# Value and output projections of two mixers as 2x2 block products with seven partial products, full-height diff scores, and a causal mask on GpSimd

## The chip, the cores and the metric

The kernel runs on one core of a Trainium2 chip. A core has a matrix engine (TensorE, in the profile PE, its weight loads PEld), a vector engine (VectorE, DVE), an engine for activation functions (ScalarE, ACT), a general one (GpSimd, POOL), and SyncE (SP), which here issues every transfer between DRAM and the on-chip memory SBUF. TensorE writes into PSUM, eight banks of 128 x 512 float32. The metric is the device time of one execution in microseconds (us).

## The reference

The reference is a two-layer decoder trunk on one sequence of 1024 tokens with 1024 features, in float32. Each layer is feed-forward, mixer, feed-forward, each between two RMS norms and added to the residual. Cut to what matters here:

```python
def hybrid_mixer(h, w_in, w_out, ...):          # layer 0
    proj = h @ w_in                              # 1024 x 3088
    dq, dk, dv, gq, gk, gv, gg, ga = split(proj) # 512 512 512 256 256 512 512 16
    a_out = diff_attention(dq, dk, dv, ...)      # 4 heads, two scores each (64 deep), values 128 wide
    o_b = gla_chunked(gq, gk, gv, log_a)         # 4 heads of linear attention, values 128 wide
    return concatenate([a_out, norm(o_b) * silu(gg)]) @ w_out

def stick_breaking(h, w_qkv, w_out):             # layer 1, 8 heads of 128
    q, k, v = split(h @ w_qkv, 3)
    ...
    mask = key < query                           # strict
    log_keep = where(mask, -softplus(z), 0)
    att = where(mask, exp(z + log_keep + suffix_sums(log_keep)), 0)
    return (att @ v) @ w_out
```

Diff attention takes softmax(score 0) - lambda * softmax(score 1) for each head, with a mask that lets a token see itself, then an RMS norm of each head's output.

## The kernel before

Every large matmul works on float32 split in two parts, `hi` and `lo` (ACT writes `hi`, VectorE `lo`, in `split`, `split_w` and `split_tile`), and takes three passes, hi·hi, hi·lo and lo·hi (`mm3`, lines 228 to 230). Tokens are worked in two halves of 512 (`TB`), features in tiles of 128 (`P`). X, the normalized input of a stage, lies transposed: eight tiles of 128 features by 512 tokens for each half.

The feed-forward stages (`gu`, `down_strassen`) already treat their products as 2x2 blocks with seven partial products (Strassen's scheme in Winograd's form): sums of X blocks on VectorE, sums of weight blocks on GpSimd, 12 quarter-size matmuls for each contraction tile. The mixers don't.

A mixer begins with `first_proj`: the first head's q and k for the first token half, then `make_x` transposes the second half's X, then the same for it. The rest of the projections are closures that the attention loops call as filler: `proj_steps` gives two steps for a 128-column tile (one for each token half, 24 matmuls 512 wide), `proj_v_steps` four for 256 value columns (48 matmuls 256 wide, with tokens as the output rows; line 771 evicts two row tiles at a time into `v`). `filled(fill, i)` spreads what is left of a head's fillers evenly over its eight blocks of 128 queries. The order of instructions on each engine is set by the framework at build time: by program order, with instructions that it expects to be ready moved ahead of those that would wait.

Layer 0 runs linear attention in two pairs of heads (`gla_pair`: a decay by gate, then seven levels in which VectorE, GpSimd and ACT make factors, TensorE multiplies and VectorE copies under a mask, then the state chain and the output), then diff attention in four heads. `diff_attn` makes for each query block and each of the two components the scores (`scores`, line 788), with two passes: one 128 rows deep that holds hi parts of q and k and lo parts of q, and one 64 rows deep for the lo part of k (`k[2]`, one tile for both components). Then come maxima (VectorE), exponentials (ACT), their combination (VectorE), transposes (line 803), the product with `v` (line 924) and the norm. Layer 1 runs eight heads of `sb_attn`: scores with three passes, two sigmoids on ACT (lines 820 and 821), a reversed running product (line 823, `TENSOR_TENSOR_SCAN`) and a product (826) on VectorE, transposes, and the product with `v` (831). In both, the causal mask is a fourth matmul on the block of the diagonal (line 791), which adds -1e30 from a bfloat16 tile.

Each head's output, transposed (`ot`, 128 x 1024), goes to DRAM (`put_o`), the last one stays. The output projection (`out_steps`, `mix_out`) runs in four parts of eight contraction tiles, 96 matmuls each: first token half by first column half in seven fillers of the last head, the rest after it. The first half's norm, residual and next X (`epilogue`, `make_x`) lie under the second half's matmuls. Weights pass through four raw buffers (`rp`, 4 KB a partition) into six split ones (`wp`).

## Time and profile before

| | us |
|---|---|
| median of 3 runs | 2507.36 (2505.67 to 2509.91) |
| the profiled execution | 2509.04 |
| its span in the profile | 2507.3 |
| granted TensorE clock in it | 0.994 of full speed |
| ACT busy | 1069.0 (43%) |
| first feed-forward | to about 361 |
| layer 0: first projections, linear, diff attention | 361 to 875 |
| layer 0: rest of the output projection | 875 to 965 |
| two feed-forwards | 965 to 1625 |
| layer 1: stick-breaking attention | 1625 to 2095 |
| layer 1: rest of the output projection | 2095 to 2182 |
| last feed-forward | 2182 to 2507 |

The stages overlap by some microseconds. In the rows below, a group of instructions is written as line, engine, operation, what is written `<-` what is read, shape and count, then `busy us, mean ns of one | idle time of the engine just before them, and what ended it`. A timeline row has the start, the duration, and the same names; a duration is that of one record (of all, where a row stands for several), and records of one engine may overlap, since the engines are pipelined. A row of the table of windows has the stretch, its length, the busy time and count of each engine, the granted clock, the share of the transfer engines and what they moved in GB/s.

### The profile page before, as it was taken

The page shows a single profiled execution, that of the slowest core. Times are in us where ns is not written, and L with a number is a line of the kernel's source. Part 1 is how long each engine was busy: PE and PEld are TensorE (multiplying, and loading weights), DVE is VectorE, ACT ScalarE, POOL GpSimd, SP SyncE. Part 2 cuts the span into 40 slices and gives each one's busy share as a digit, 9 for nine tenths or more (in the row PEclk, how much of TensorE's full clock was granted, in tenths as well). Part 3 has the DMA queues.
Part 4 walks back from the last instruction along what each step waited for, and adds up shares of the span by engine and source line. Part 5 has one row for each costly group of instructions (what it writes and reads, how often), then busy time and mean ns, then how long its engine had stood idle before and what let it go on. Part 6 is the DMA issues. An engine that isn't in the chain of part 4 may idle for free.

```text
span 2507.3 us, 32918 instructions
## 1 busy us (share of the span) xinstructions
PE 2430.2 (97%) x12253; PEld 1995.7 (80%) x12253; DVE 1733.3 (69%) x2635; ACT 1069.0 (43%) x2143; POOL 671.2 (27%) x542
## 2 busy tenths in 40 slices
PE   7999999999999999999989999999999999999998
PEld 6887878788777678887868887788888988888776
DVE  6768786653656758777888678855546476686778
ACT  6423454322545646323455234543323254552343
POOL 2545431110000012545423455310000000043553
PEclk9999999999999999999999999999999999999999
DMA  5321651211100354233463225531111024422245
GB/s 171 84 81 61 213 185 47 68 46 65 34 30 35 105 184 128 76 85 108 161 197 84 78 65 187 170 101 34 41 36 35 30 100 160 151 83 84 63 158 196
DMA packets 238842, 251.97 MB, mean 100 GB/s; under 512 B 9861, under 2 KB 186201, under 8 KB 238681
## 3 DMA queue, kind: packets, MB, share of 16 engines
q1 hardware_dynamic: 238680, 249.85, 31.3%
q8 instruction: 97, 1.59, 0.3%
q14 instruction: 65, 0.52, 0.1%
HBM read 215.21 MB, written 34.60 MB: 100 GB/s over the span
## 4 chain that ended last, share of the span: by engine, by line
PE 82%; DVE 10%; issue 3%; POOL 2%; ACT 2%; DMA 2%; DVEq 0%; SPq 0%; POOLq 0%; ACTq 0%
PE z L788 4%; PE pps L228 4%; PE pps L230 4%; PE pps L229 4%; PE pd L228 3%; PE pd L230 3%; PE pd L229 3%; PE pa L230 3%; PE pa L228 3%; PE pa L229 3%; PE pc L229 3%; PE pc L230 3%; PE pc L228 3%; PE vps L228 3%; PE po L831 2%
## 5 line engine op out<-in xcount | busy, mean ns | idle before, releaser
L182 POOL TENSOR_TENSOR rs<-ms,nhalf 128x1 f32<-128x1 f32 (+1 forms) x136 | 100.2, 743 | 1046.1 <-DVE ms L180 950.4
L277 ACT CAST wq<-rawt 128x512 fp32r<-128x512 f32 x264 | 163.3, 621 | 351.4 <-PE pc L230 164.3
L278 DVE TENSOR_TENSOR wq<-rawt,wq 128x512 fp32r<-128x512 f32 x264 | 242.8, 924 | 22.6 <-ACT wq L277 16.7
L219 DVE TENSOR_TENSOR hl<-rawd,hl 128x512 fp32r<-128x512 f32 x200 | 166.2, 834 | 86.6 <-ACT hl L218 86.3
L218 ACT CAST hl<-rawd 128x512 fp32r<-128x512 f32 x200 | 123.7, 621 | 208.5 <-issue 46.7
L228 PE MATMUL pps<-hl,wh 128*128 128x512 f32 x512 | 206.6, 404 | 0.3 <-DVE hl L222 0.3
L230 PE MATMUL pps<-hl,wl 128*128 128x512 f32 x512 | 203.1, 397 | 0.0
L229 PE MATMUL pps<-hl,wh 128*128 128x512 f32 x512 | 202.7, 396 | 0.0
L371 POOL TENSOR_TENSOR rawt<-rawt 128x512 f32<-128x512 f32 x44 | 72.0, 1636 | 395.9 <-DMA rawt<-in_ffn_w_up_dram 184.9
L228 PE MATMUL pd<-hl,wq 128*128 128x512 f32 x352 | 139.9, 397 | 10.7 <-DVE c L385 10.7
L228 PE MATMUL vps<-vh,hl 128*128 128x256 f32 x512 | 146.9, 287 | 0.0
L805 DVE COPY att<-tps 128x512 f32<-128x512 f32 (+2 forms) x96 | 56.4, 587 | 129.6 <-PE tps L803 129.0
L230 PE MATMUL vps<-vh,hl 128*128 128x256 f32 x512 | 145.1, 283 | 0.0
L229 PE MATMUL vps<-vl,hl 128*128 128x256 f32 x512 | 144.8, 283 | 0.0
L228 PE MATMUL pa<-hl,wq 128*128 128x512 f32 x352 | 138.7, 394 | 4.1 <-DVE hl L222 3.4
L230 PE MATMUL pa<-hl,wq 128*128 128x512 f32 x352 | 138.1, 393 | 4.1 <-DVE wq L278 4.1
L788 PE MATMUL z<-k,q 128*128 128x512 f32 (+5 forms) x444 | 140.0, 396 | 1.8 <-ACT b L821 1.0
L228 PE MATMUL pc<-hl,wq 128*128 128x512 f32 x352 | 137.6, 391 | 3.1 <-ACT hl L218 3.1
L230 PE MATMUL pd<-hl,wq 128*128 128x512 f32 x352 | 139.6, 396 | 0.0
L229 PE MATMUL pd<-hl,wq 128*128 128x512 f32 x352 | 139.4, 396 | 0.0
L230 PE MATMUL pc<-hl,wq 128*128 128x512 f32 x352 | 138.3, 393 | 0.0
L229 PE MATMUL pc<-hl,wq 128*128 128x512 f32 x352 | 138.3, 393 | 0.0
(281 smaller groups left out, 6684.4 us busy)
## 6 DMA issues: line engine op xcount, KB each, us to landing
rawt<-in_ffn_w_gate_dram SPq DMA_DIRECT2D x88, 512.0 KB, 4.0
rawd<-in_ffn_w_down_dram SPq DMA_DIRECT2D x60, 512.0 KB, 3.7
rawd<-in_ffn_w_down_dram SPq DMA_DIRECT2D x116, 256.0 KB, 2.7
rawt<-in_ffn_w_up_dram SPq DMA_DIRECT2D x44, 512.0 KB, 4.0
hres<-h SPq DMA_DIRECT2D x40, 512.0 KB, 2.9
h<-hres SPq DMA_DIRECT2D x40, 512.0 KB, 5.1
rawt<-in_hyb_w_in_dram SPq DMA_DIRECT2D x16, 512.0 KB, 3.9
rawt<-in_sb_w_qkv_dram SPq DMA_DIRECT2D x16, 512.0 KB, 3.8
```

What stands on the lines that cost most here:

```text
L182: nc.gpsimd.tensor_tensor(out=rs, in0=ms, in1=self.nhalf.to_broadcast([P, n]) if n > 1 else self.nhalf, op=ALU.pow)
L218: nc.scalar.copy(out=t[:, 0], in_=src)
L219: nc.vector.tensor_tensor(out=t[:, 1], in0=src, in1=t[:, 0].bitcast(F32), op=ALU.subtract)
L228: nc.tensor.matmul(ps, lhsT=ah, rhs=bh, start=first, stop=False, skip_group_check=more)
L229: nc.tensor.matmul(ps, lhsT=ah, rhs=bl, start=False, stop=False, skip_group_check=more)
L230: nc.tensor.matmul(ps, lhsT=al, rhs=bh, start=False, stop=last, skip_group_check=more)
L277: nc.scalar.copy(out=w[:, 0], in_=src)
L278: nc.vector.tensor_tensor(out=w[:, 1], in0=src, in1=w[:, 0].bitcast(F32), op=ALU.subtract)
L371: gt(out=b11, in0=b12, in1=b11, op=ALU.subtract)
L788: nc.tensor.matmul(z[:, :wide], lhsT=lhs[:, i * P:(i + 1) * P], rhs=rhs[:, c0:c0 + wide], start=j == 0, stop=j == len(passes) - 1 and not ...
L805: (nc.scalar.copy if j0 else nc.vector.tensor_copy)(out=t[:, :n], in_=ps[:, :n])
L831: nc.tensor.matmul(po, lhsT=v[:, j, hv:hv + P], rhs=at, start=j == 0, stop=j == i)
```

## The change

*Value rows.* A new stage `values` runs at the start of each mixer, in place of `first_proj`. It computes the 1024 value columns (layer 0: 512 of diff attention and 512 of linear attention) for all tokens as a 2x2 block product, and stores the rows in a DRAM tile `vd`. `load_v` fetches 256 columns (1 MB) as they are needed. `proj_v_steps` is gone from all fillers, and `proj_steps` gives four half steps of 12 matmuls instead of two of 24. `Blocks` loads weight blocks and forms the sums t1 to t4 on GpSimd (1, 2, 1 and 3 operations).

```diff
+class Blocks:
+    def load(self, *places):
+        r = self.t.rp.tile([P, 2, TB], F32, name="rawd", tag="raw")
+        for i, (k, c) in enumerate(places):
+            self.t.nc.sync.dma_start(out=r[:, i], in_=self.w[self.rows(k), self.cols[c]])
+        return r
...
+    def t1(self, j):
+        r = self.load((j, 0), (j, 1))
+        self.sub(r[:, 0], r[:, 1], r[:, 0])
+        return r[:, 0]
+    def t2(self, j):
+        r = self.t1(j)
+        b = self.b22(j)
+        self.sub(b, b, r)
+        return b
...
+    def t4(self, j):
+        r = self.t1(j)
+        b = self.load((j + self.KH, 0), (j + self.KH, 1))
+        self.sub(b[:, 0], b[:, 0], b[:, 1])
+        self.sub(r, b[:, 0], r, ALU.add)
+        return r
...
+    def values(self, l, w, cols, X, xn1, vd):
...
+        pa = self.new_accs("va")
+        self.rows_product(pa, A[0:4], weights(B.b11), True)
+        for t in range(NTT):
+            nc.scalar.copy(out=u2[t], in_=pa[t])
+        self.rows_product(pa, A[4:8], weights(B.b21), False)
+        for t in range(NTT):
+            out(0, 0, t, lambda o: nc.scalar.copy(out=o, in_=pa[t]))
...
+        R = self.make_raw(xn1, "mix_pre_g", l, xr)
+        X.append([self.split(r, self.hp) for r in R])
...
+        for j in range(4):
+            tt(out=s12[j], in0=R[j], in1=R[j + 4], op=ALU.add)
+            S1.append(self.split(s12[j], sp))
+            tt(out=s12[j], in0=s12[j], in1=hi(j), op=ALU.subtract)
+            tt(out=s12[j], in0=s12[j], in1=lo(j), op=ALU.subtract)
+            S2.append(self.split(s12[j], sp))
+        pb = self.new_accs("vb")
+        self.rows_product(pb, S2, weights(B.t2), True)
+        for t in range(NTT):
+            tt(out=u2[t], in0=pb[t], in1=u2[t], op=ALU.add)
+        pc = self.new_accs("vc")
+        self.rows_product(pc, S1, weights(B.t1), True)
...
+        self.rows_product(pc, S4, weights(B.b22), False)
...
+        pd = self.new_accs("vd")
+        self.rows_product(pd, S3, weights(B.t3), True)
...
+        self.rows_product(pd, X[1][4:8], weights(B.t4), False)
```

*Output projection.* `out_steps` now gives eight fillers of 12 matmuls: the products A11·b11 and S3·t3 (S3 = first minus second token half). `mix_out` loads the seven stored heads again (`orw`), forms S1, S2 and S4 on GpSimd and runs the other five products, b21, t2, t1, b22 and t4, with the first half's norm and next X between the last two.

```diff
+        for j in range(4):
+            gt(out=o[j][1], in0=o[j][1], in1=o[j + 4][1], op=ALU.add)
+            gt(out=o[j][0], in0=o[j][1], in1=o[j][0], op=ALU.subtract)
+        pa = self.new_accs("oa")
+        product(pa, lambda j: o[j + 4][0], B.b21, True)
...
+        product(pb, lambda j: o[j][0], B.t2, True)
...
+        product(pc, lambda j: o[j][1], B.t1, True)
...
+        product(pc, lambda j: o[j + 4][0], B.b22, False)
...
+        for t in range(NTT):
+            gt(out=c22[t], in0=c22[t], in1=p7[t], op=ALU.add)
+            gt(out=u2[t], in0=u2[t], in1=p7[t], op=ALU.add)
+        xn0 = self.epilogue(0, fo[0], ss[0], False, hsrc, hdst, False)
+        nxt0 = self.make_x(xn0, gname, gi, self.xp)
+        pd = self.new_accs("od")
+        product(pd, lambda j: o[j + 4][1], B.t4, True, tail=4)
```

*Scores.* In diff attention the lo part of k gets a tile of its own for each component, filled in both row halves (one more ACT copy for each, 16 in all), and the second pass is 128 rows deep. In stick-breaking attention the mask matmul goes; GpSimd writes the diagonal block of both sigmoids instead.

```diff
-                zs = self.scores([(q[c], k[c]), (q[c][r], k[2][r])], i, "incl")
+                zs = self.scores([(q[c], k[c]), (q[c], k[2 + c])], i, "incl")
...
-            zs = self.scores([(q[:, 0], k[:, 0]), (q[:, 0], k[:, 1]), (q[:, 1], k[:, 0])], i, "strict")
+            zs = self.scores([(q[:, 0], k[:, 0]), (q[:, 0], k[:, 1]), (q[:, 1], k[:, 0])], i, None)
...
+            for t, fill_with in ((a, 1.0), (b, 0.0)):
+                nc.gpsimd.affine_select(out=t[:, n - P:n], in_=t[:, n - P:n], pattern=[[-1, P]],
+                                        compare_op=ALU.is_ge, fill=fill_with, base=-1, channel_multiplier=1)
```

Besides, the tile of post-norm gains moves to a pool of its own and some constants share a buffer; in `gla_pair` the fillers are spread evenly over its four output pieces.

More of the change, by code (lines that the diff above doesn't have):

```diff
@@ L671, in down_strassen, with rows_product @@
         return nxt0, self.epilogue(1, fo1, ss[1], True, hsrc, hdst, nxt is None)
+    def rows_product(self, accs, As, Bs, start, tail=1):
+        n = len(As)
+        m = max(0, n - tail)
+        seq = [(j, t) for j in range(m) for t in range(NTT)] + [(j, t) for t in range(NTT) for j in range(m, n)]
+        for j, t in seq:
+            ts = slice(t * P, (t + 1) * P)
+            self.mm3(accs[t], As[j][:, 0, ts], As[j][:, 1, ts], Bs[j][:, 0], Bs[j][:, 1],
+                     start and j == 0, j == n - 1, more=not start)
@@ L1045, in gla_pair @@
                                         .to_broadcast([P, 4, P]), op=ALU.mult)
-                fill[2 * h + c4]()
+                for _ in range(len(fill) // (4 - 2 * h - c4)):
+                    fill.pop(0)()
                 pt = self.zp.tile([P, 4, P], F32, name="got", tag="z")
@@ new lines, in out_steps, with mix_out @@
+        self.begun = B, order, st
+        return [lambda n=n: step(n) for n in range(8)]
+    def mix_out(self, l, hsrc, hdst, gname, gi):
+        nc = self.nc
+        tt, gt = nc.vector.tensor_tensor, nc.gpsimd.tensor_tensor
+        B, order, st = self.begun
+        C = B.cols
+        wp = self.wp_tag()
+        pg = self.load_pg(self.a["mix_post_g"][l])
+        cx = ExitStack()
+        orw = self.dyn(cx, "orw", KD - 1)
+        o = []
+        for j in range(KD):
+            if j == KD - 1:
@@ L1198, in prep @@
                 r = self.olast
             else:
-                r = self.rp.tile([P, S], F32, name="rawo", tag="raw")
-                self.nc.sync.dma_start(out=r, in_=self.ot[l][order[f]])
-            for tb in range(2):
-                O[tb].append(self.split(r[:, tb * TB:(tb + 1) * TB], self.hp if tb else self.xp))
-        accs = []
-        def step(f):
-            if not accs:
-                accs.extend(self.acc.tile([P, TB], F32, name="dps%d" % t, tag="acc") for t in range(NTT))
-            prep(f)
-            self.down_step(w, order[f], O[0], f, KD, accs)
@@ new lines, in product @@
+        def product(accs, a, b, start, tail=1):
+            As, Bs = [], []
+            for j in range(4):
+                As.append(self.split(a(j), self.hp))
+                Bs.append(self.split(b(j), wp))
+            self.rows_product(accs, As, Bs, start, tail)
+        for j in range(4):
+            gt(out=o[j][1], in0=o[j][1], in1=o[j + 4][1], op=ALU.add)
+            gt(out=o[j][0], in0=o[j][1], in1=o[j][0], op=ALU.subtract)
+        pa = self.new_accs("oa")
+        product(pa, lambda j: o[j + 4][0], B.b21, True)
@@ L1227, in mix_out @@
+        for t in range(NTT):
+            c = fo[1][t][:, C[0]]
+            tt(out=c, in0=pd[t], in1=u2[t], op=ALU.add)
+            gained(c, 1, t, 0)
+        xn1 = self.epilogue(1, fo[1], ss[1], False, hsrc, hdst, False)
+        cx.close()
+        self.octx.close()
         self.hctx.close()
```

284 lines of the change are left out of this document (181 added, 103 removed).

## The prediction

> **What bounds the kernel now.** I read the first part of the page, then the groups by line, then TensorE's timeline for the real pace of its matmuls, then VectorE's timeline beside GpSimd's, and last the table of windows for the stages that change.
>
> ```profile
> span 2507.3 us, 32918 instructions
> PE 2430.2 (97%) x12253; PEld 1995.7 (80%) x12253; DVE 1733.3 (69%) x2635; ACT 1069.0 (43%) x2143; POOL 671.2 (27%) x542
> ```
>
> TensorE is busy for 97% of the span, so the first question is what the change does to its queue. The durations of the groups mislead here, because a matmul's record runs past the start of the next one. The pace is the distance between starts:
>
> ```profile
> L228 PE MATMUL vps<-vh,hl 128*128 128x256 f32 x512 | 146.9, 287 | 0.0
> L228 PE MATMUL dps<-hl 128*128 128x512 f32 x256 | 101.9, 399 | 0.0
> 361.41 0.39 PE L228 MATMUL pps<-hl,wh 128*128 128x512 f32 x1
> ...
> 372.10 0.39 PE L230 MATMUL pps<-hl,wl 128*128 128x512 f32 x1
> ...
> 597.60 0.28 PE L229 MATMUL vps<-vl,hl 128*128 128x256 f32 x1
> ...
> 603.12 0.28 PE L230 MATMUL vps<-vh,hl 128*128 128x256 f32 x1
> ```
>
> The first pair is the first and last of 48 matmuls 512 wide: 10.69 us over 47 steps, 0.2274 us each. The second is the first and last of 47 that are 256 wide: 5.52 us over 46 steps, 0.120 us. So the 256-wide value projection, whose duration of 287 ns looks dear beside 399 ns, is only 5% dearer per column.
>
> **TensorE's part of the sum.** Value projection: three groups (L228 to L230) of 512, 1536 matmuls at 0.120 us, 184.3 us. After: seven products of 4 row tiles by 4 contraction tiles by 3 passes, 336 matmuls a layer, 672 at 0.2274 us, 152.8 us. Saved: **31.5 us**, not the 170 us that durations would suggest. Output projection: 768 matmuls (three groups of 256) become 672, 96 x 0.2274 = **21.8 us** saved.
>
> ```profile
> L788 PE MATMUL z<-k,q x192: 274/436/505, 635.6 to 874.9; 128*128 128x512 f32 x40, 64*128 64x512 f32 x40, 128*128 128x256 f32 x32, 64*128 64x256 f32 x32
> 722.34 1.42 PE L788 MATMUL z<-k,q 128*128 128x384 f32 x4
> 723.69 0.23 PE L791 MATMUL z<-mkb_incl,identb 128*128 128x128 bf16 x1
> ...
> 2066.61 1.14 PE L788 MATMUL z<-k,q 128*128 128x384 f32 x6
> 2067.59 0.23 PE L791 MATMUL z<-mkb_strict,identb 128*128 128x128 bf16 x1
> 2067.63 0.48 PE L228 MATMUL dps<-hl 128*128 128x512 f32 x1
> ```
>
> Diff scores: of 192 matmuls half contract 64 rows only. At 722.34 a block of 640 keys takes two full and two 64-row passes (384 and 256 wide) and 1.35 us; at 2066.61 stick-breaking attention takes the same widths in six full passes and 0.98 us, 0.163 us a pass. So each 64-row pass costs (1.35 - 4 x 0.163) / 2 = 0.35 us more than a full one. With K=128 everywhere, 96 x 0.35 = **33.5 us** go. The Trainium skill ("TensorE: Matmul & The Clock Gate", section "Why this matters for your kernels") says that a single K=32 matmul takes as long as a K=128 one; by that nothing would go. The rows above disagree.
>
> Mask: 64 matmuls leave stick-breaking attention, 0.04 us each (2067.59 to 2067.63): **2.6 us**.
>
> ```profile
> PE xps L210 <- DVE xn L193: 4.3, 5, 1.7
> 40.41 3.49 PE xps L268 x32
> ```
>
> The mixers' second half of X is transposed 32 times before and after (3.5 us), but now the first product needs the first half alone and stands ahead of it for 96 x 0.2274 = 21.8 us, so that wait goes: **4 us**. TensorE's queue together: 31.5 + 21.8 + 33.5 + 2.6 + 4 = **93 us** less.
>
> **What the seven products ask of VectorE and GpSimd.** This is where I expect much of it to be given back.
>
> ```profile
> 319.19 1.88 DVE L648 TENSOR_TENSOR fo<-dc,u 128x512 f32<-128x512 f32 x3
> ...
> 263.54 0.68 DVE L219 TENSOR_TENSOR hl<-ph,hl 128x512 fp32r<-128x512 f32 x1
> 263.86 1.51 POOL L566 TENSOR_TENSOR rawd<-rawd 128x512 f32<-128x512 f32 x1 [0.79 <-DVE hl L219]
> ...
> 264.21 1.71 DVE L219 TENSOR_TENSOR hl<-t,hl 128x512 fp32r<-128x512 f32 x1
> ```
>
> Three 512-wide VectorE operations in a row take 1.88 us: a pace of (1.88 - 0.68) / 2 = 0.60 us. One that reads two SBUF operands while GpSimd works takes 1.71 us instead of 0.68, 1.03 us more, and ends about when GpSimd's ends. What that costs on average is seen in the feed-forward down products, which already have this form:
>
> ```profile
> L219 DVE TENSOR_TENSOR hl<-rawo,hl 128x512 fp32r<-128x512 f32 x28 | 18.4, 684 | 0.0
> L219 DVE TENSOR_TENSOR hl<-rawd,hl 128x512 fp32r<-128x512 f32 x200 | 166.2, 834 | 86.6 <-ACT hl L218 86.3
> L219 DVE TENSOR_TENSOR hl<-ph,hl 128x512 fp32r<-128x512 f32 x136 | 125.4, 934 | 0.0
> L566 POOL TENSOR_TENSOR rawd<-rawd 128x512 f32<-128x512 f32 x40 | 57.7, 1451 | 36.9 <-DMA rawd<-in_ffn_w_down_dram 34.3 <-DVE hl L219 2.4
> ```
>
> Against 684 ns without GpSimd (rawo), 200 x 0.150 + 136 x 0.250 = 64 us were added; the code has 35 GpSimd operations in each down stage (10 of L566), 140 in all. That is 0.46 us per GpSimd operation, my value, since that stage is the nearest; the ends are 0.2 and 1.03.
>
> *Values stage, each layer.* VectorE has 52 splits, 28 combinations and 20 PSUM evictions, 100 operations; 92 of them come after the second half of X is there: 55.2 us, and 28 GpSimd operations add 12.9, so 68 us. TensorE then has some 5 us of the first product left, the transposes, and five products of 48 matmuls (10.9 us each): 63 us. Stall 5 us, two layers **10 us** (ends 0 and 42). What is late there is S2 for the third product: it waits behind eight splits of X and the S1 tiles.
>
> *Output stage, each layer.*
>
> ```profile
> L475 DVE SCALAR_TENSOR_TENSOR h<-fo,rs,h 128x1024 f32<-128x1024 f32 x32 | 42.9, 1359 | 10.7 <-POOL rs L182 10.7
> L193 DVE TENSOR_SCALAR fo<-h,rs 128x1024 f32<-128x1024 f32 x28 | 21.1, 753 | 10.0 <-POOL rs L182 9.7
> L222 DVE SCALAR_TENSOR_TENSOR hl<-xps,gcol,hl 128x512 fp32r<-128x512 f32 x64 | 43.3, 743 | 2.5 <-ACT hl L221 2.5
> 905.00:965.00 60.00, 59.53 (x276) 48.80 (x275) 38.60 (x71) 33.45 (x65) 9.31 (x13) 1.00 0.58 186
> ```
>
> The window shows the stage now: TensorE never waits, VectorE is at 64%, and the 192 matmuls of the second row half, 43.7 us, hide the first half's normalization. After: 40 splits, 20 evictions, 16 gains at 0.60 us (45.6), eight rows of 1.36 + 0.75 (16.9), eight splits of the next X (5.9), 68.4 us, and 44 GpSimd operations add 20.2: 88.6 us. Seven splits and ten GpSimd operations (8.8 us) can go ahead of the last head's end, and twelve operations and four rows of the second half (15.6 us) can lie under the feed-forward's first columns. Left: 64.2 us, against 5 x 10.9 + 3.5 - 8.2 (three quarters of the first product done as filler) = 49.9 us. Stall 14 us, two layers **29 us** (ends 7 and 67). It falls between the last two products: only t4's 10.9 us cover the first half's normalization. The seven loads of the stored heads go to SP ahead of the weights; what is left of their landing I count in the upper end.
>
> *Transfers.* A values stage loads 56 x 256 KB and stores 16 x 256 KB, 18.9 MB in some 85 us, 222 GB/s.
>
> ```profile
> 250.00:260.00 10.00, 10.00 (x46) 8.29 (x45) 5.48 (x9) 5.27 (x10) 2.57 (x2) 1.00 0.81 290
> ```
>
> 290 GB/s is seen without a wait of TensorE, so I cost it at nothing; four raw buffers, two to a t4, are the cover, and if they don't do, each t4 costs its load and three GpSimd operations instead of 2.7 us. The value rows go through DRAM: each 1 MB comes back one head pair early, or under the eight half steps of the first projections (21.8 us), so that costs nothing too; bare, it would be 3.6 us at that rate, eight times.
>
> **The attention stages lose filler.**
>
> ```profile
> 400.00:425.00 25.00, 25.00 (x199) 23.91 (x199) 16.40 (x33) 11.75 (x18) 2.10 (x2) 1.00 0.07 22
> 440.00:465.00 25.00, 23.61 (x133) 19.92 (x134) 21.35 (x27) 6.96 (x8) 2.24 (x2) 1.00 0.13 43
> 650.00:905.00 255.00, 250.77 (x1338) 189.00 (x1338) 167.13 (x394) 137.44 (x383) 19.58 (x33) 1.00 0.18 63
> L730 ACT CAST k<-pps 64x512 fp32r<-64x512 f32 x16 | 9.3, 581 | 7.1 <-DVE k L713 6.9
> L127 POOL TENSOR_SCALAR_AFFINE_SELECT mk_strict<-mk_strict 128x128 f32<-128x128 f32 x1 | 0.3, 319 | 0.0
> 2078.17 0.63 PE L803 MATMUL tps<-ident,b 128*128 128x128 f32 x4 [0.63 <-DVE b L826]
> ...
> 2085.88 0.30 PE L803 MATMUL tps<-ident,b 128*128 128x128 f32 x1 [0.90 <-DVE b L826]
> ```
>
> Linear attention: the 25 us at 400 are covered by value matmuls that leave. The gate projections, now in the next stretch, can come forward, and that stretch is VectorE's anyway (21.35 of 25). I take **6 us** (ends 0, and 16 if the 16.4 us of VectorE's chain lie bare). Diff attention: TensorE falls from 255 us to about 200 (33.5 us of short passes and 23 us of values go), VectorE stays near 165 and ACT gets 16 more casts of 0.581 us; half of those (5 us) and two waits a head as in the last two rows, 6 us, make **11 us** (ends 0 and 28). Stick-breaking attention: the last head, which is filled with 12 matmuls a block as all heads will be, waits 0.63 + 0.90 us; seven heads 10.7 us. Its queue is fuller than the others' will be, but the two selects (0.32 us) now stand in the chain before the scan, and the scans and transposes queue behind them. **8 us** (ends 0 and 20).
>
> **The sum.** The profiled execution took 2509.0 us, 1.7 above its span; the median shown is 2507.4. Saved 93, given back 10 + 29 + 6 + 11 + 8 = 64: 29 less, 2480 in that execution's terms and **2478** against the median.
>
> **The rivals.** *A, all is covered.* VectorE's backlog sinks under the projections behind the values stage and under the feed-forward; the attention costs (25 us) stay: 2507.4 - 93 + 25 = 2439. For it: the down products run with hardly a wait. Against: they have five or six contraction tiles per eviction, these have four. *B, slower: the port.* If VectorE stands for the whole of nearly every GpSimd operation, 1.03 us, the values stage is 84 us against 63 and the output stage 83.6 against 49.9: stalls 42 and 67, and with 25 that is 134 against 93, 2548. The sign turns at 0.70 us per GpSimd operation, since each 0.1 costs 12 us. For it: 264.21. Against: the mean of 0.46. The Trainium skill ("SBUF — State Buffer", section "Who interferes with whom") states B's rule, an exclusive pair that an operation holds to its end; the single rows agree, the mean shows how seldom they meet. *C, K=128 saves nothing* (the change doesn't do what it says there, because the dear part is changing operands, not the 64 rows): 2478 + 33.5 = 2511. *D, the attention stages starve:* their upper ends, 64 instead of 25, 2517.
>
> **How the numbers follow.** The forecast has 0.48, with a range of its own of 2445 to 2510; A 0.14, B 0.16, C 0.06, D 0.11, and 0.05 is something else. A measurement of this kernel tells about 0.2%, 5 us. Faster: 0.43 + 0.14 + 0.03 + 0.03 = 0.63; same 0.09; slower 0.28. The range goes from A (2438) to just below B (2535).
>
> **What would show it.** Right: the 64-row passes gone from the scores, and blocks of diff attention 0.7 us (up to 512 keys) or 1.4 us shorter; TensorE idle before S2's product on `hl` from VectorE, and before the last product or its transposes; VectorE near 90% in both stages, its two-operand splits well over 0.684 us. Wrong: TensorE waiting on DMA in the output stage, VectorE under 80% there, or idle time in most heads of stick-breaking attention.

## The result, and the profile after

The forecast was wrong in sign. The changed kernel takes **2645.0 us** (median, 2639.9 to 2645.8) against 2508.6 beside it: a ratio of 1.054, 95% interval 1.052 to 1.056. That is 136 us slower, and outside the range of 2438 to 2535.

The first part of the page of the changed kernel, each engine's busy time, share of the span and instructions:

```profile
span 2644.1 us, 32215 instructions
PE 2386.2 (90%) x11229; PEld 1930.7 (73%) x11229; DVE 1933.5 (73%) x2866; ACT 1130.2 (43%) x2263; POOL 996.6 (38%) x820
```

TensorE has 1024 matmuls fewer and is busy 44 us less, while the span grew by 137: it now waits. VectorE's share rises only from 69% to 73%. Nothing on this page looks like a bound; the stages do.

In this table a stage begins with its first matmul in the trace. "Beyond the pace" is its length less its matmuls at the paces of the prediction (0.227 us at 512 columns, 0.120 at 256, and likewise 0.172 at 384, 0.11 at 128 and 0.04 for the bfloat16 matmuls of the mask); it is what TensorE waits or loses.

| stage | before, us | beyond the pace | after, us | beyond the pace |
|---|---|---|---|---|
| layer 0: first projections; after, with values | 28.4 | 3.0 | 137.8 | 36.1 |
| linear attention | 245.8 | 26.8 | 180.7 | 30.8 |
| diff attention | 252.5 | 47.5 | 219.0 | 44.0 |
| output projection behind the last head | 63.6 | 1.6 | 104.0 | 45.8 |
| layer 1: first projections; after, with values | 51.7 | 3.3 | 138.2 | 36.4 |
| stick-breaking attention | 414.6 | 24.0 | 382.6 | 61.8 |
| output projection behind the last head | 72.6 | 1.6 | 103.2 | 45.0 |

The four feed-forwards keep their length within 3 us. In the mixers the matmul time falls by 26.6 + 29.2 = 55.8 us; what lies beyond it grows by 192.1.

The waits view of the changed kernel, for TensorE: what it waited for, us in total, times, the longest:

```profile
PE xps L262 <- DVE fo L245: 47.5, 7, 23.4
PE vb L280 <- ACT hl L270: 34.3, 3, 16.6
PE tps L919 <- DVE b L946: 30.2, 32, 4.9
PE oc L280 <- DVE c L1400: 17.7, 2, 9.3
...
PE vd L280 <- DVE vo L811: 9.4, 2, 4.7
PE oa L280 <- ACT hl L270: 6.9, 2, 6.3
```

Six rows hold 146 us. In the profile before, the waits of the first and third for the same VectorE operations come to 3.2 us, and the others aren't there. `vb` is the second product of the values, `oc` the third product of the output, `xps` the transposes for the next X behind the output's first half, `tps` the transposes of the weights in stick-breaking attention.

The timeline of the changed kernel around these waits, first in the values stage, then in the output stage (start, duration, engine, line, what is written; idle before it in brackets):

```profile
394.37 2.50 DVE L781 TENSOR_TENSOR s<-xr 128x512 f32<-128x512 f32 x4 [2.83 <-ACT xr L322]
396.79 8.12 DVE L271 TENSOR_TENSOR hl<-xr,hl 128x512 fp32r<-128x512 f32 x8
404.83 0.68 DVE L271 TENSOR_TENSOR hl<-s,hl 128x512 fp32r<-128x512 f32 x1
...
408.63 0.79 PE L280 MATMUL vb<-hl 128*128 128x512 f32 x1 [16.48 <-ACT hl L270]
...
938.65 7.48 POOL L61 TENSOR_TENSOR rawd<-rawd 128x512 f32<-128x512 f32 x4 [10.00 <-DMA rawd<-in_hyb_w_out_dram]
945.59 1.09 DVE L271 TENSOR_TENSOR hl<-rawd,hl 128x512 fp32r<-128x512 f32 x1 [4.36 <-ACT hl L270]
946.60 2.47 DVE L1400 TENSOR_TENSOR c<-oc,u 128x512 f32<-128x512 f32 x4
947.42 0.76 PE L280 MATMUL oc<-hl 128*128 128x512 f32 x1 [8.33 <-DVE c L1400]
958.70 6.87 POOL L61 TENSOR_TENSOR rawd<-rawd 128x512 f32<-128x512 f32 x5
966.25 0.69 DVE L271 TENSOR_TENSOR hl<-rawd,hl 128x512 fp32r<-128x512 f32 x1 [3.14 <-ACT hl L270]
967.47 1.88 DVE L1404 TENSOR_TENSOR fo<-oc,u 128x512 f32<-128x512 f32 x3
...
983.50 0.90 PE L262 MATMUL xps<-ident,fo 128*128 128x128 f32 x3 [22.68 <-DVE fo L245]
```

Two things are to be seen. At 394, eight splits of X (8.12 us where they would take 4.9 at 0.60 each) and the sums stand between the second half's X and the product that needs only S2. At 945 and 966, VectorE's queue is in order: the eviction at 946.60 belongs to matmuls of which the last began at 938.7, but a weight split is ahead of it that waits, through ScalarE, for GpSimd's sums. The evictions at 967.47, of matmuls of which the last began at 960.4, are late for the same reason, and only then does the residual and norm chain start, 16 us long, to the transposes at 983.50.

The same stretches in the table of windows (busy us of each engine, granted clock, DMA share, GB/s), of the changed kernel:

```profile
360.00:490.00 130.00, 101.36 (x431) 80.19 (x431) 86.23 (x129) 47.21 (x84) 55.66 (x38) 0.91 0.61 191
392.00:445.00 53.00, 34.25 (x140) 26.71 (x139) 48.79 (x69) 24.74 (x45) 21.00 (x9) 0.84 0.35 112
445.00:498.00 53.00, 48.24 (x201) 38.94 (x200) 17.29 (x26) 8.46 (x12) 18.25 (x14) 0.94 0.82 249
392.00:408.60 16.60, 0.15 (x2) 0.00 (x0) 14.23 (x19) 10.92 (x22) 5.57 (x4) 0.62 0.48 161
408.60:413.00 4.40, 4.37 (x10) 3.06 (x11) 4.40 (x8) 0.72 (x2) 3.35 (x1) 0.51 0.44 142
890.00:1002.00 112.00, 71.12 (x301) 57.54 (x302) 74.08 (x106) 42.97 (x90) 59.68 (x45) 0.80 0.48 166
897.00:904.00 7.00, 0.33 (x1) 0.14 (x1) 0.41 (x1) 0.86 (x2) 1.59 (x2) 0.79 1.00 382
```

VectorE is at 66% in both stages (86 of 130, 74 of 112) and TensorE at 78% and 64%: neither fills the stage. But VectorE's work lies unevenly: 48.8 of the 53 us behind the second half's X, 17.3 of the next 53. The last row is the start of the output stage: all engines nearly idle, TensorE for 6.3 us, and the transfers full at 382 GB/s, while the stored heads and the first weights come in together.

### The profile page after: what moved, and what is told of

The parts are those of the page before. It is cut to its first block, busy times and chain, and to the rows that moved or that the text cites. A ratio compares the mean times of both kernels' runs of the same rounds, so it can differ in the third digit from the quotient of the medians.

```text
span 2644.1 us, 32215 instructions
## 1 busy us (share of the span) xinstructions
PE 2386.2 (90%) x11229; PEld 1930.7 (73%) x11229; DVE 1933.5 (73%) x2866; ACT 1130.2 (43%) x2263; POOL 996.6 (38%) x820
## 4 chain that ended last, share of the span: by engine, by line
PE 55%; DVE 15%; issue 12%; POOL 8%; DMA 6%; ACT 3%; SPq 1%; POOLq 0%; DVEq 0%; ACTq 0%
DVE hl L271 4%; PE pd L280 3%; PE pd L281 3%; PE pd L282 3%; PE pc L281 3%; PE pc L282 3%; PE pc L280 3%; POOL rawd L61 3%; PE pa L282 3%; PE pa L280 3%; PE pa L281 3%; POOL rs L234 2%; PE pps L280 2%; PE pps L282 2%; PE pps L281 2%
## 5 line engine op out<-in xcount | busy, mean ns | idle before, releaser
L271 DVE TENSOR_TENSOR hl<-rawd,hl 128x512 fp32r<-128x512 f32 x248 | 218.9, 886 | 139.2 <-ACT hl L270 138.8
L270 ACT CAST hl<-rawd 128x512 fp32r<-128x512 f32 x248 | 153.3, 622 | 345.6 <-POOL rawd L61 144.9
L234 POOL TENSOR_TENSOR rs<-ms,nhalf 128x1 f32<-128x1 f32 (+1 forms) x136 | 105.8, 785 | 410.6 <-DVE ms L232 340.2
L330 DVE TENSOR_TENSOR wq<-rawt,wq 128x512 fp32r<-128x512 f32 x264 | 240.5, 916 | 12.2 <-ACT wq L329 6.3
L61 POOL TENSOR_TENSOR rawd<-rawd 128x512 f32<-128x512 f32 x112 | 177.4, 1591 | 177.9 <-DMA rawd<-in_sb_w_qkv_dram 47.2
L280 PE MATMUL pd<-hl,wq 128*128 128x512 f32 x352 | 139.8, 397 | 10.7 <-DVE c L437 10.7
L280 PE MATMUL pa<-hl,wq 128*128 128x512 f32 x352 | 139.4, 396 | 3.2 <-DVE hl L274 3.2
L282 PE MATMUL pa<-hl,wq 128*128 128x512 f32 x352 | 138.6, 395 | 3.5 <-DVE wq L330 3.2
L281 PE MATMUL pa<-hl,wq 128*128 128x512 f32 x352 | 138.5, 394 | 0.0
L940 POOL TENSOR_SCALAR_AFFINE_SELECT a<-a 128x128 f32<-128x128 f32 x64 | 24.5, 384 | 285.0 <-ACT a L936 263.2
L904 PE MATMUL z<-k,q 128*128 128x512 f32 (+2 forms) x480 | 125.8, 374 | 4.4 <-ACT e L1019 3.7
L271 DVE TENSOR_TENSOR hl<-ph,hl 128x512 fp32r<-128x512 f32 x136 | 126.5, 941 | 0.0
```

What stands on the lines that cost most here:

```text
L61: self.t.nc.gpsimd.tensor_tensor(out=out, in0=a, in1=b, op=op)
L234: nc.gpsimd.tensor_tensor(out=rs, in0=ms, in1=self.nhalf.to_broadcast([P, n]) if n > 1 else self.nhalf, op=ALU.pow)
L270: nc.scalar.copy(out=t[:, 0], in_=src)
L271: nc.vector.tensor_tensor(out=t[:, 1], in0=src, in1=t[:, 0].bitcast(F32), op=ALU.subtract)
L280: nc.tensor.matmul(ps, lhsT=ah, rhs=bh, start=first, stop=False, skip_group_check=more)
L281: nc.tensor.matmul(ps, lhsT=ah, rhs=bl, start=False, stop=False, skip_group_check=more)
```

## The experiments

Four kernels first split the change into its parts.

**k128**: before, with only the diff scores' second pass 128 rows deep (and what makes room for the tiles: the gains tile and some constants move, and one pool of the attention goes from four buffers to three).

```diff
-            zs = self.scores([(q[c], k[c]), (q[c][r], k[2][r])], i, "incl")
+            zs = self.scores([(q[c], k[c]), (q[c], k[2 + c])], i, "incl")
...
+                self.nc.scalar.copy(out=L[c][o, cs], in_=L[c][r, cs].bitcast(F32))
```

> The kernel before with only the second pass of the diff scores made 128 rows deep (a lo tile of k for each component, eight k buffers, and the moves of the gains tile and constants that make room). If a 64-row pass costs 0.35 us more than a full one and TensorE bounds diff attention: about 2476 us (-33). If what was dear was the change of operands and not the 64 rows: 2508. If the casts on ACT and the shorter cover take half of it back: 2490.

Measured: 2488.2 us, ratio 0.992 (0.991 to 0.994): 19 us faster. Diff attention falls from 252.5 to 231.6. The block of 640 keys that the prediction priced, in the timeline of this kernel:

```profile
712.62 0.83 PE L790 MATMUL z<-k,q 128*128 128x384 f32 x4
713.29 0.23 PE L793 MATMUL z<-mkb_incl,identb 128*128 128x128 bf16 x1
```

Four passes in 0.67 us, where they took 1.35: 0.34 us for each short pass, the unit price of the prediction. But all recorded score passes of the stage together, from one start to the next, fall from 68.0 to 43.2 us, 24.8, not 33.5. A pair of passes gains 0.28 us on average at 256 and 384 columns and only 0.22 at 512, and 40 of the 96 pairs are 512 wide. At 256 columns the medians before were 0.294 us for the full pass of a pair and 0.313 for the short one; here they are 0.200 and 0.122. And the stage gains less than its passes: 2.5 of its 20.9 us are matmuls of the output projection that now run behind the last head. Beyond the pace, the first three heads fall by 19.1 us, the last, whose fillers are those output steps, not at all (13.1 before, 13.7 here).

**mask**: before, with only the causal mask of stick-breaking attention on GpSimd.

```diff
-            zs = self.scores([...], i, "strict")
+            zs = self.scores([...], i, None)
...
+            for t, fill_with in ((a, 1.0), (b, 0.0)):
+                nc.gpsimd.affine_select(out=t[:, n - P:n], in_=t[:, n - P:n], ...)
```

> The kernel before with only the mask of stick-breaking attention on GpSimd (two selects for each block, no mask matmul). Serial-chain theory: the selects lie ahead of the scan, but the 24-matmul fillers of the kernel before cover them, so 2506 to 2511. Small-step theory, with the mask as its main part: the stage goes from 415 us towards the 383 + 92 of the changed kernel's, so 2520 to 2535.

Measured: 2506.6 us, ratio 0.9996 (0.9986 to 1.0006), no difference. The stage goes from 414.6 to 411.7 us, about the 2.6 us of its mask matmuls; the selects in the chain cost nothing that shows.

**outonly**: before, with only the new output projection (`out_steps`, `mix_out`, `Blocks`). **oldout**: the changed kernel with the old output projection.

> The kernel before with only the output projection as seven products. Serial-chain theory: the stretch from the last head to the next feed-forward grows by 40 us in layer 0 and 31 us in layer 1 as in the changed kernel, so 2580 us. Rival (the output stage only suffers from what the other parts left behind): under 2530.

> The changed kernel with the old output projection. If the loss of that part is its own, 2645 - 75 = 2570 us; if the parts share one bound (VectorE with GpSimd on its port), less comes back: over 2600.

Measured: outonly 2603.3 us, ratio 1.038 (1.037 to 1.040), 96 us slower, 23 more than its first expectation; oldout 2545.1, ratio 1.015 (1.013 to 1.016), 37 us slower and below both of its expectations. With 19 for k128 that makes the values stage and what goes with it 57 us slower. The parts add up: 96 + 57 - 19 = 134, of 136. Both block products lose; the output loses more.

The next four ask why.

**nosum**: the changed kernel without the sums of weight blocks.

```diff
     def sub(self, out, a, b, op=ALU.subtract):
-        self.t.nc.gpsimd.tensor_tensor(out=out, in0=a, in1=b, op=op)
+        pass
```

> The changed kernel with the sums of weight blocks on GpSimd left out: each product reads the first raw block in place of the sum (the values are then not the reference's). All loads, splits, matmuls and evictions stay. Chain theory (TensorE idles because the work between two products is a serial chain on VectorE and ScalarE with no matmuls beside it): the 16.6 us gap before the second product of the values and most of the 22.8 us gap before the transposes in the output stage stay, because their chains hold few GpSimd sums; the 8.5 us gap inside the third output product goes, since that chain ran through a late sum; 2600 to 2625 us. Port theory (112 GpSimd sums of 1.59 us take VectorE's time one for one, and VectorE is the bound of both stages): nearly all of the extra idle time of these stages goes, some 2 x 33 + 2 x 44 us, less what the matmuls need: 2500 to 2530 us.

Measured: 2572.0 us, ratio 1.026 (1.025 to 1.028). The 112 sums cost 73 us, 0.65 each. Between the two theories: the values stages fall by 16.6 and 15.9 us, the output stages by 8.2 and 14.2, stick-breaking attention by 10.8; in layer 0 the wait before `vb` falls only from 16.5 to 12.2 us, the one before the transposes from 22.7 to 21.9, and the one inside the third output product from 8.3 to 2.2. So the sums are half of the loss, and the two long waits are mostly something else.

**vlate**: the changed kernel with the splits of the second half's X behind the third product's eviction.

```diff
-        X.append([self.split(r, self.hp) for r in R])
...
         for t in range(NTT):
             tt(out=c22[t], in0=pc[t], in1=u2[t], op=ALU.add)
+        X.append([self.split(r, self.hp) for r in R])
```

> The changed kernel with one thing in the values stage later: the eight splits of the second token half's X are written behind the third product's eviction, instead of ahead of the sums that the second product needs. Same work. Chain theory: the gap before the second product falls from 16.6 us to some 9 us in each mixer, as these splits took 8.1 us in front of it; 2 x 7 us less, 2628 to 2636 us. Port theory: VectorE and GpSimd have the same work in the stage, and the stage keeps its length within 3 us: 2640 to 2648 us.

Measured: 2648.7 us, ratio 1.056 (1.054 to 1.058): no gain. The wait before `vb` falls from 16.5 to 11.7 us, somewhat less than the chain theory has it, and the stage stays at 138.6 us in layer 0: six waits of 1.0 to 2.6 us stand in the later products, 10.2 in all, where the changed kernel has three of 6.9 together, and the rest comes back as slower matmuls. The chain theory fails here. Its timeline shows what VectorE meets while GpSimd sums:

```profile
393.98 1.75 DVE L271 TENSOR_TENSOR hl<-rawd,hl 128x512 fp32r<-128x512 f32 x1
395.65 1.75 DVE L782 TENSOR_TENSOR s<-s,hl 128x512 f32<-128x512 f32 x1
397.32 1.75 DVE L271 TENSOR_TENSOR hl<-rawd,hl 128x512 fp32r<-128x512 f32 x1
399.00 0.68 DVE L783 TENSOR_TENSOR s<-s,hl 128x512 f32<-128x512 f32 x1
```

Three GpSimd sums run from 393.62 to 398.53. Each VectorE operation that starts beside them takes 1.75 us, the next one 0.68.

**oswap**: the changed kernel with the last output product ahead of the first half's residual and norm.

```diff
+        pd = self.new_accs("od")
+        product(pd, lambda j: o[j + 4][1], B.t4, True, tail=4)
+        xn0 = self.epilogue(0, fo[0], ss[0], False, hsrc, hdst, False)
         for t in range(NTT):
             gt(out=c22[t], in0=c22[t], in1=p7[t], op=ALU.add)
             gt(out=u2[t], in0=u2[t], in1=p7[t], op=ALU.add)
-        xn0 = self.epilogue(0, fo[0], ss[0], False, hsrc, hdst, False)
         nxt0 = self.make_x(xn0, gname, gi, self.xp)
-        pd = self.new_accs("od")
-        product(pd, lambda j: o[j + 4][1], B.t4, True, tail=4)
```

> The changed kernel with the last output product (48 matmuls, 10.9 us) placed ahead of the first token half's residual and norm chain, and the eight GpSimd additions of the seventh product behind that chain's start. Same work. Chain theory: these 10.9 us of matmuls now run beside the chain, and the 22.8 us gap before the transposes falls by 8 to 14 us, shared with a new wait for the last product's operands; 2 x 8 to 2 x 14 us less, 2615 to 2630 us. Port theory: VectorE and GpSimd have the same work, the stage keeps its length within 3 us: 2639 to 2648 us.

Measured: 2644.0 us, ratio 1.055 (1.053 to 1.057): nothing. The waits view for TensorE in this stage of oswap:

```profile
PE xps L262 <- DVE fo L245: 7.1, 2, 6.5
...
PE pa L280 <- DVE hl L274: 2.7, 1, 2.7
PE od L280 <- ACT hl L270: 2.4, 1, 2.4
```

The wait before the transposes falls from 22.7 to 6.5 us, most of it by the product's own 10.9, which now lies there; the stage gains 5 us (104.0 to 98.7, 103.2 to 98.4), and the feed-forwards behind it lose 3.9 and 2.4. Behind layer 0 most of it is lost in the first 40 us: after a wait of 2.7 us before `pa` (in the rows above) eight of the next matmuls come some 0.43 us apart instead of 0.227. That the second half's chain has lost its cover doesn't show: its transposes wait 1.2 us here and 0.9 in the changed kernel.

**late**: oldout with q and k in whole steps of 24 matmuls.

```diff
-        return [lambda tb=tb, kh=kh: step(tb, kh) for tb in range(2) for kh in range(2)]
+        return [lambda tb=tb: (step(tb, 0), step(tb, 1)) for tb in range(2)]
```

> The changed kernel with the old output projection (2545.1 us before this edit), and the projections of q and k given to the attention loops in whole steps of 24 matmuls again, so that the spreading rule places four of them at the last four query blocks of a head instead of a half step at each of the eight. Same matmuls. Placement theory (the stick-breaking attention lost its time because the last blocks, whose chains are longest, now have 12 matmuls to cover them instead of 24): the two waits of 1.3 us per head at the last blocks shrink, stick-breaking attention falls from 365 us by 10 to 18 us, diff attention by 0 to 4; 2525 to 2535 us. Cover theory (the value projections that left the loops are missed as cover wherever the rest is placed): waits move to the early blocks, and the time stays within 4 us of 2545. GpSimd theory (the mask on GpSimd and the extra copies are what holds it): no change either.

Measured: 2533.7 us, 11.4 less than oldout; stick-breaking attention 365.3 to 351.6. The placement theory holds. TensorE's wait in the same stretch of the stage, first oldout, then late:

```profile
PE tps L919 <- DVE b L946: 21.0, 28, 1.1
```

```profile
PE tps L919 <- DVE b L946: 3.4, 8, 1.1
```

Four steps over eight query blocks fall on the last four, whose chains are long; eight half steps fall one on each block, and the last blocks have 2.7 us of cover for a chain that needs more.

Three more weigh the price of the sums.

**t2keep**: the changed kernel with the second product's sums kept for the fourth operand.

```diff
     def t4(self, j):
-        r = self.t1(j)
-        b = self.load((j + self.KH, 0), (j + self.KH, 1))
-        self.sub(b[:, 0], b[:, 0], b[:, 1])
-        self.sub(r, b[:, 0], r, ALU.add)
+        r = self.load((j + self.KH, 0))[:, 0]
+        self.sub(r, r, self.kept[j])
         return r
```

> The changed kernel with the second product's weight sums kept, so that the last product's operand is one load and one GpSimd sum instead of two loads and three sums: per product of seven, 8 of 28 sums and 4 x 3 of the loads of 256 KB in the last product go (to pay for the room, the values stage has 3 row buffers on their way to DRAM instead of 4). With all sums left out the changed kernel took 2572.0 us, 73 less; 8 of 28 of that is 21 us. GpSimd theory (each sum costs about its share, through the port and through late operands): 2615 to 2630 us, and VectorE's wait ahead of the last product's splits in the values stage, 4.8 us of TensorE in each mixer, goes. Chain theory (the two long gaps of 16.6 and 22.8 us are other chains, and the sums of the last product lie beside them): 2635 to 2645 us.

Measured: 2607.7 us, ratio 1.040 (1.039 to 1.042): 37 us less, more than the 21 of its share and below both expected ranges. The output stages fall by 12.0 and 7.3 us, stick-breaking attention by 9.4. The wait in the values' last product, which was to go, falls from 4.7 to 2.7 us in layer 0 and stays at 4.6 in layer 1. The wait before the transposes falls from 22.7 to 14.6 us, because the evictions ahead of the norm no longer come late. That need not be the work of the sums, since this edit takes away loads too. In nosum, with no sums at all, the same evictions came 6 us after their last matmul began (930.06), behind a weight split of the next feed-forward that waited for its load:

```profile
935.07 0.62 ACT L329 CAST wq<-rawt 128x512 fp32r<-128x512 f32 x1 [5.42 <-DMA rawt<-in_ffn_w_gate_dram]
935.72 0.69 DVE L330 TENSOR_TENSOR wq<-rawt,wq 128x512 fp32r<-128x512 f32 x1 [5.35 <-ACT wq L329]
936.32 1.88 DVE L1404 TENSOR_TENSOR fo<-oc,u 128x512 f32<-128x512 f32 x3
```

So VectorE's queue makes the evictions late in both kernels, once behind t4's sums (958.70), once behind a load. With the sums on VectorE and all loads in place (vsum, below) the wait is 16.3 us. What stands ahead of the evictions changes from build to build, and no run divides t2keep's gain between fewer sums and fewer loads.

**vsum**: the changed kernel with the sums on VectorE.

```diff
-        self.t.nc.gpsimd.tensor_tensor(out=out, in0=a, in1=b, op=op)
+        self.t.nc.vector.tensor_tensor(out=out, in0=a, in1=b, op=op)
```

> The changed kernel with the 112 weight sums on VectorE instead of GpSimd, one word of the code. On GpSimd a sum takes 1.59 us and stretches a VectorE operation beside it from 0.68 to 1.75 us; on VectorE it takes about 0.6 us. Port theory (the sums cost VectorE more from the neighbour than they would on itself): VectorE's time in the two stages falls by 112 x 0.4 = 45 us, and the time by 20 to 40 us: 2605 to 2625. Load theory (VectorE is the bound, and any work added to its queue lengthens the stages): slower, by up to 112 x 0.6 = 67 us: 2645 to 2690.

Measured: 2590.8 us, ratio 1.033 (1.031 to 1.035): 54 us less, with VectorE given 112 operations more. Its load theory (any work added to VectorE lengthens the stages) is out; the gain is above the 20 to 40 us that the port theory gave. The groups by line, first after, then vsum (busy us, mean ns, idle before):

```profile
L271 DVE TENSOR_TENSOR hl<-rawd,hl 128x512 fp32r<-128x512 f32 x248 | 218.9, 886 | 139.2 <-ACT hl L270 138.8
L61 POOL TENSOR_TENSOR rawd<-rawd 128x512 f32<-128x512 f32 x112 | 177.4, 1591 | 177.9 <-DMA rawd<-in_sb_w_qkv_dram 47.2 <-DMA rawd<-in_hyb_w_in_dram 35.0 <-DMA rawd<-in_hyb_w_out_dram 34.7
```

```profile
L271 DVE TENSOR_TENSOR hl<-rawd,hl 128x512 fp32r<-128x512 f32 x248 | 200.7, 812 | 58.8 <-ACT hl L270 57.6 <-PE va L282 0.7
L61 DVE TENSOR_TENSOR rawd<-rawd 128x512 f32<-128x512 f32 x112 | 80.1, 722 | 21.4 <-DMA rawd<-in_sb_w_qkv_dram 7.4 <-DMA rawd<-in_hyb_w_in_dram 6.2 <-DMA rawd<-in_hyb_w_out_dram 3.8
```

On VectorE a sum takes 0.72 us instead of 1.59. Its time beside GpSimd shrinks a little (0.886 to 0.812 us a weight split); what shrinks most is VectorE's idle time ahead of these splits, 139 to 59 us: it no longer stands at the head of its queue for a sum that comes late. So both are at work, the port and the lateness, and this run does not divide the 54 us between them. The pages of the changed kernel and of nosum bound the port: with the same 2866 operations VectorE is busy for 1933.5 and 1903.2 us, so the sums stretch its operations by 30 us, 0.27 us a sum, where leaving them out saves 73.

**kmask**: before, with both parts that need no block products.

> Before with both parts that need no block products: the 128-row second pass in the diff scores and the causal mask of stick-breaking attention on GpSimd. If the two parts do not touch each other, 2488.2 less 0.9: 2485 to 2490 us, and what separates it from the changed kernel, some 157 us, is all of the two block-product stages and of what they did to the attention loops. If the copies and the mask share a wait, 2490 to 2500.

Measured: 2487.0 us, ratio 0.993 (0.991 to 0.995). The two parts don't touch each other. It equals k128 within the noise, and these two are the only versions that are faster than both kernels.

What was open then is whether the causes are separate, and what the block products cost when the repairable ones are gone.

**allfix**: the changed kernel with the edits of vsum, t2keep and late. **valfix**: the same with the old output projection. **valfix2** and **allfix2**: these two with the edits of vlate and oswap.

> The changed kernel with the weight sums on VectorE, the second product's sums kept, and whole steps of 24 matmuls for q and k: three edits measured at -54, -37 and -11 us one by one. If they are separate causes: 2645 - 102 = 2543 us. If the first two are mostly the same time (sums on GpSimd; with no sums at all it was 2572, only 19 less than with sums on VectorE, and keeping them takes 12 of 28 of that, 8 us): 2645 - 54 - 8 - 11 = 2572 us. By the chain theory the two long gaps remain in both, some 12 and 16 us a mixer, so that it stays above the 2507.5 of before.

> The same three edits with the old output projection: the values alone as block products. With whole steps it was 2533.7 us; the sums on VectorE took 10 us from each values stage, the kept sums 1 to 4 more: 2505 to 2513 us, so that the block products of the values, which save 31 us of matmuls, still cost some 20 us more than before with K=128 and mask (2487.0). If the stage becomes bound by TensorE instead, 2475 to 2487 us.

> The previous kernel with the eight splits of the second half's X behind the third product's eviction, which moved nothing while GpSimd's sums ran beside it (2648.7 against 2645.0 us). Chain theory: with VectorE free of its neighbour the shorter chain before the second product is worth 4 us a mixer, 8 us less than the previous kernel. Load theory: the splits only wait later, within 3 us of it.

> The first kernel of this group with the last output product ahead of the residual and norm chain, which moved nothing with the sums on GpSimd: the gap of 22.8 us fell to 6.7, but 10.9 us of it were the product's own, other waits of 5 us came in the stage, and the next feed-forward began 4 us later. Chain theory: with the operands earlier it is now worth 4 to 8 us a mixer, 8 to 16 us less. Conservation (the second half's own chain loses the cover that the first one gains): within 4 us.

| | us | ratio to before (95%) |
|---|---|---|
| allfix | 2556.5 | 1.019 (1.018 to 1.021) |
| valfix | 2508.4 | 1.000 (0.999 to 1.001) |
| valfix2 | 2509.8 | 1.001 (1.000 to 1.002) |
| allfix2 | 2558.7 | 1.020 (1.018 to 1.022) |

allfix gains 88 of the 102 us of its three edits one by one, halfway between its two expectations: largely separate causes, with an overlap of 14. (Kept sums take 8 of 28, as in t2keep's expectation, not the 12 that allfix's says.) Against kmask, valfix is 21 us slower, so the values as block products still lose, and the block output loses 48 more. The two order edits again moved nothing, now without a neighbour on the port. The middle of the values stage shows why, in the table of windows of valfix and then of valfix2:

```profile
392.00:445.00 53.00, 41.70 (x173) 33.68 (x174) 52.41 (x87) 23.03 (x41) 1.84 (x2) 0.87 0.39 121
```

```profile
392.00:445.00 53.00, 42.07 (x155) 32.62 (x156) 50.59 (x83) 22.10 (x39) 1.85 (x2) 0.84 0.36 116
```

From the second half's X to the fourth product VectorE is busy for 52.4 and 50.6 of 53 us, while TensorE has 42; eight or nine of its operations there are weight sums. Whatever stands first in that queue, 53 us of it have to pass; this is the load theory of valfix2, and the chain theory falls for the values. In the output, allfix2 does shorten the stage (93.0 to 88.1, 91.1 to 85.6) and the feed-forwards behind nearly give it back (behind layer 0, from the first `pa` to the first `da`, 221.5 to 225.2; behind layer 1, from the first `pa` to the last `dd`, 329.9 to 334.4). As in oswap, the first matmuls behind the wait of 2.7 us before `pa` come 0.43 us apart (from 964.75), and the first 40 us of that feed-forward are 5.2 us beyond the pace, 1.0 in allfix.

## Why the prediction was wrong, step by step

**TensorE's matmul time: right.** Value and output projections and mask were 31.5 + 21.8 + 2.6 = 55.9 us; the count of the trace at the same paces gives 55.8. That a 256-wide matmul is nearly as cheap per column was read from the pace, and it was so.

**The 64-row passes: the kind right, the sum too high.** 33.5 us forecast, 24.8 in the passes, 19 in the kernel. The price of one block, 384 and 256 columns wide, was multiplied by 96, and the average pair cost less (0.28 us, and 0.22 at 512 columns); in the last head the stage gained nothing. Rival C (nothing is saved) is out. The Trainium skill's sentence beside it is about a single matmul, which no run here times; in the kernel before, the full pass of a pair was slow as well (0.294 us at 256 columns, beside 0.313), so the price belongs to the pair and not to the 64-row pass alone.

**The first X: right, and worth nothing.** The waits of 4.3 us are gone; 2.4 us for ScalarE's evictions stand in the same place, and behind the transposes TensorE waits 16.5 us for the next product.

**The values stage: the step that failed first.** "Stall 5 us", 10 for two layers (ends 0 and 42), came from all of VectorE's operations behind the second half's X (68 us) against all of TensorE's matmuls behind it (63 us). Measured: 33 us more beyond the pace in each stage, 66 together. The sum treated the operations as if they could be done at any time. In the trace they aren't spread over 63 us: VectorE can start none before the transposes, is busy for 48.8 of the next 53 us while TensorE has 34.2, and in the 53 us behind that is busy for 17.3 and idle for 17 behind ScalarE's casts, which wait for GpSimd's sums of weights. That S2 would wait behind eight splits of X was seen and written down, and was then priced by the difference of two totals.

**The output stage: the same step, larger.** 14 us forecast, 44 measured in each layer, 88 together where the upper end was 67. (At 0.2 us a sum its lower end is 11, not 7.) Three waits make most of it: 6.3 us at the start for the heads' loads, in layer 0 alone (1.0 in layer 1), which were left in the upper end; 8.3 and 9.3 us where an eviction stood behind a split that waited for t4's first sums; and 22.7 and 23.4 us before the transposes. Of these last, 16 are the chain of residual and norm (967.47 to 983.50; 16 in nosum and t2keep too), under which no matmul lies, and some 7 are again the queue. The text said that only t4's product covers the first half's normalization; in the trace it lies behind the transposes and covers nothing of it. When it is put ahead (oswap, allfix2) the stage gains 5 us, and the kernel nothing.

**Transfers: costed at nothing, and that is not shown to hold.** In the values stage of layer 0 GpSimd waits 35.0 us for weight blocks, 11 times, and SyncE, which issues the loads, waits 44.7 us, 12 times, for VectorE's splits to give a raw buffer back. TensorE doesn't wait for these loads directly; late sums and evictions pass it on. No run changes the loads alone, so how much of the 136 us this is stays open.

**GpSimd's price: undersized, not the cause of the sign.** 0.46 us a sum from the feed-forward; nosum gives 0.65. At 0.65 the prediction's own sum would have ended some 20 us higher, about at 2500. Rival B named the right neighbour, and its sign turned at 0.70; but it priced one mechanism, VectorE slowed beside a sum. That one alone is 0.27 us a sum here, less than forecast; what was left out is the sum that comes late. Half of the loss stays with no sums at all, and the other half is the port and the lateness in an in-order queue together. The Trainium skill ("SBUF — State Buffer", section "Who interferes with whom") says that a VectorE operation with two SBUF inputs contends with a GpSimd operation that reads SBUF; the rows at 393.98 (1.75 us, then 0.68) agree. What queues behind the blocked one was in no term of the sum.

**Stick-breaking attention: 8 us forecast, 37.8 measured.** By the runs: 13.7 for the half steps (beyond the pace, 46.4 in oldout and 32.7 in late), 15.4 with the new output steps in place of the old ones (61.8 in after, 46.4 in oldout), 9.0 for the values that left (32.7 against kmask's 23.7). The first was priced from the last head's two waits, 10.7 us, and is near; the second was not in the sum. Of it 9.6 us are in the last head (6.4 to 16.0): the splits and sums of the new output steps were charged to the output stage alone, not to the last head, in whose queues they stand. The other 5.8 us lie in heads without such steps, and no run says why; in outonly, with the old fillers, the whole stage is only 3 us more beyond the pace. The two selects cost nothing (mask).

**Linear attention: near. Diff attention: near by luck.** 6 and 11 us forecast, 4 and, against k128's 29.0, 15 measured. The two waits a head for lost filler, 6 of the 11, don't show: without the new output steps the stage is at 27.3 (oldout), below k128's 29.0. All of the 15 are the output steps, which were in no term: 16.6 us more in the last head (11.4 to 28.0), and as much in outonly (13.1 to 30.2).

The signs named as "wrong" all came: TensorE waiting on DMA in the output stage, VectorE at 66% there, and idle time in most heads of stick-breaking attention. Of the signs named as "right", VectorE near 90% in both stages did not come. The others did: the short passes gone, and the longest waits before S2's product and before the transposes, so the places were right and the sizes were not. What remains open is the division of vsum's 54 us between port and lateness, and whether a product placed beside the 53 us in the values stage (q and k of the first token half) would pay; it wasn't tried.

## What to carry to other kernels

Compare the totals of two engines only over the stretch in which the work can be done: from the arrival of the last input to the product that needs it, not over a stage. Before an operation moves to a slower engine, ask who stands in an in-order queue behind its consumer; a late sum, or a late load, holds up evictions that have nothing to do with it. A block product saves an eighth of the matmuls, but its first half of the tokens needs five of the seven products: where the next stage's norm was hidden under the other half's matmuls, count what is left to hide it.

## What the runs showed of the hardware

A long wait costs more than its length. After 16.5 us of idle, the first nine matmuls of `vb` start 0.41 to 0.59 us apart instead of 0.227, from 408.63 to 412.92, at a granted clock of 0.51; then the pace is back. That is 4.3 us for some 2 us of work. Behind the other long wait, in the table of windows of the changed kernel, the 32 transposes take 7 us, where 0.11 us each would be 3.5:

```profile
983.50:990.40 6.90, 6.54 (x31) 5.50 (x32) 4.92 (x9) 5.84 (x14) 1.37 (x2) 0.55 0.99 357
```

The Trainium skill ("TensorE: Matmul & The Clock Gate", section "HAM oscillation — how this bites in real kernels") says that an idle gap of over some 3.4 us brings the half clock back; the rows of 408.60 and 983.50 agree, with waits of 16.5 and 22.7 us, and 4.3 us is what the return took here. Shorter waits did it too in these runs, though not each time, so 3.4 us is no lower bound here. The same line of the feed-forward waited 2.68 us at 1218.57 and 2.70 us at 1560.72 in the changed kernel: after the first, matmuls came 0.43 us apart for six steps, after the second at the full pace:

```profile
1218.57 0.76 PE L280 MATMUL pd<-hl,wq 128*128 128x512 f32 x1 [2.68 <-DVE c L437]
1219.13 0.63 PE L281 MATMUL pd<-hl,wq 128*128 128x512 f32 x1
...
1560.72 0.47 PE L280 MATMUL pd<-hl,wq 128*128 128x512 f32 x1 [2.70 <-DVE c L437]
1561.02 0.40 PE L281 MATMUL pd<-hl,wq 128*128 128x512 f32 x1
```

The prediction counted no such loss.

A sum of two 128x512 tiles takes 1.59 us on GpSimd in these stages and 0.72 on VectorE, and moving 112 of them to the busier engine made the kernel 54 us faster.
